# Seven block products in place of eight in the second product of the second layer's MLP, in token order

## The chip, the cores and the metric

The kernel runs on one core of a Trainium2 chip. The metric is the device time of one execution in microseconds (us). Before the change the median of three runs is 1055.32 us. A core has TensorE (PE, matrix products; PEld is its loading of the stationary operand), VectorE (DVE), ScalarE (ACT), GpSimd (POOL), and SyncE (SP), whose queue issues nearly all transfers here. Each engine works through its own queue in order and waits at its head for what it needs from the others. Products go into PSUM, which the kernel uses as eight banks of 128 x 512 numbers of 32 bits.

## The reference

Two layers work on 512 tokens of 1024 features. The first mixes tokens by Fourier groups and attention, the second by pooling. After its mixer each layer has an MLP, and the change touches the second layer's only:

```python
def sq_relu_mlp(u, w1, w2):
    a = jnp.maximum(u @ w1, 0.0)
    return (a * a) @ w2

h = h + g1 * y
h = h + g2 * sq_relu_mlp(modulate(rms_norm(h, norm2_g[l]), sh2, sc2), w_mlp1[l], w_mlp2[l])
```

Here u is 512 x 1024, w1 is 1024 x 4096, w2 is 4096 x 1024, and g2 is a row of 1024 gates, the modulation row v = 5 of the layer. All data are float32. The result of the second layer is the output.

## The kernel before

**Tiling.** The stream h lies transposed in SBUF: eight tiles `hT[d]` of 128 features by 512 tokens. Each matrix operand is split into a high part that the fast matrix format holds exactly and a low part, the rest; a product is made of three (`mm3`, lines 99 to 103): high by high, high by low, low by high, into the same PSUM bank.

**MLP.** `mlp` (line 1305 on) goes over four chunks c4 of 1024 hidden columns. In each, the first product makes eight tiles of hidden features (q = 0 to 3, m = 0, 1), 24 matmuls each; `act` (lines 1296 to 1303) squares the positive part and splits it. The second product makes eight tiles d of output features: weights as the stationary operand, hidden tiles `ah` as the moving one. `add_h` (line 855) adds a finished bank times the gate to `hT[d]`. In the last chunk `emit` turns each finished tile back to token order, four transposes on TensorE, and stores it.

**Weights.** `Feed` loads pieces of 128 x 1024 numbers (512 KB) in the order of their use, at most `nr` = 4 at a time (`load`, line 145 issues). `one` takes the next one: ScalarE casts it to its high half (`wh`, line 167), VectorE subtracts to get the low half (`wl`, line 170). There is room for eight split pieces, five in one pool and three in another; `done` gives a place back when a product has been written out in the program. `tick`, called after every second step of a product and after each `act`, takes at most one piece of weights, and only one whose load was issued over 4 us before by the program's own count.

**Order.** `manual_schedule` makes each engine issue in the order in which the program is written. Nothing overtakes: what is written ahead on VectorE is done ahead on VectorE. PSUM banks come in three classes: "m" with three, "s" with three, "t" with two.

**Buffers.** After attention, pool `M` holds "v" 16 tiles (activations in two parts), "a", "x" (three scratch tiles), "y", "z" and the band table.

Of the kernel before, what the change touches and what calls it, by code (L numbers as in the profile page):

```python
# [27 lines left out]
# columns of the constant block  # L28
# [4 lines left out]
# token windows (first token, first output, end of outputs) of the pooling products  # L33
# [5 lines left out]
def body(ctx: ExitStack, tc: tile.TileContext, x, c, cx, c_ctx, w_mod, b_mod, norm1_g, norm2_g,  # L39
         w_in, w_four, q_g, k_g, rpb, w_out, w_pool, pool_scale, w1, w2, kconst, kfour, kband, out):  # L40
    nc = tc.nc
    # every engine issues in the order in which the program is written
# [22 lines left out]
    class Slots:  # L65
        """tiles by class; one class never waits for another"""
# [8 lines left out]
    # ---------------------------------------------------------------- small jobs between the large products  # L75
# [33 lines left out]
    # ---------------------------------------------------------------- weights  # L109
# [3 lines left out]
    class Feed:  # L113
        """4 KB pieces in the order of their use: weights, which become two exact halves, and modulation rows, which are
        accumulated off the tensor engine"""

        def __init__(self, nr):
# [8 lines left out]
            # slow: the low parts of weights wait for a later moment  # L126
# [6 lines left out]
        def w(self, key, src, a, b):  # L133
            self.items.append(["w", key, src, (P, a, b), None, 0.0])
# [18 lines left out]
        def one(self, kind, auto=True, eng=None):  # L153
            """takes the next piece of a kind; nothing when there is none or no room for it"""
            if not self.wait[kind]:
                return False
            _, key, _, shape, raw, _ = it = self.wait[kind][0]
            if kind == "w":
                room = [h for h in self.halves if h[1] > 0]
# [6 lines left out]
                self.wait[kind].pop(0)  # L166
                nc.scalar.copy(hi, raw)  # L167

                def low():
                    (eng or nc.vector).tensor_tensor(lo, raw, hi.bitcast(F32), op=ALU.subtract)  # L170
# [9 lines left out]
            else:  # L180
                self.mac(key, raw)
                it[4] = None
# [6 lines left out]
        def beat(self):  # L189
            """what has had the time to arrive"""  # L190
# [22 lines left out]
        def need(self, l, v):  # L213
            """the columns of a modulation row, now"""
# [21 lines left out]
        def finish(self):  # L236
            (l, v), self.fin = self.fin, None
            ps = bank("t", "pmv")
# [5 lines left out]
            later(lambda: self.columns(l, v, ms), 7.0 if l or v == 5 else 1.5)  # L244

# [16 lines left out]
    W = Feed(4)  # L262
# [41 lines left out]
    # ---------------------------------------------------------------- constants and small parameters  # L304
# [42 lines left out]
    # silu of both conditioning vectors  # L347
# [9 lines left out]
    # ---------------------------------------------------------------- norms  # L357
# [6 lines left out]
    def rows(r, n):  # L364
        """token values in columns -> the same row on every partition"""
# [18 lines left out]
    # ---------------------------------------------------------------- transposed residual stream  # L384
# [29 lines left out]
    # ---------------------------------------------------------------- first modulation, in column chunks  # L414
# [19 lines left out]
    def mod_cols(j, ms):  # L434
# [3 lines left out]
        # md[j][:, block, shift or scale, token kind]  # L438
# [19 lines left out]
    # GEMM operands in window order: token = 128 * (column block) + 16 * row + column in block  # L458
# [83 lines left out]
    # ---------------------------------------------------------------- remaining parameters  # L542
# [6 lines left out]
    # Fourier tables  # L549
# [7 lines left out]
    # relative position table, sheared over the 16 columns of a query block  # L557
# [10 lines left out]
    def head_sums(sqs):  # L568
        """1 / rms of every head of every token tile"""
# [1017 lines left out]
```

## Time and profile before

| | |
|---|---|
| median of three runs | 1055.32 us (1054.09 to 1056.67) |
| span of the profiled execution | 1051.1 us |
| mean granted TensorE clock | 0.993 |
| instructions | 14034 |
| second layer's MLP, about | 691 us to the end |
| second product of its first chunk | 738.26 to 781.78 us |

The span runs from the first to the last instruction of the one execution that was profiled; the timed runs contain what lies around it as well. Rows of a timeline give the start, the duration, the engine, the line, the operation with output and inputs, and in brackets the idle time ahead of it with what ended it. Rows of groups give busy time, mean nanoseconds of one, and idle time ahead of the group with what ended most of it. Matmuls overlap, so the distance between two starts says more than a duration.

### The profile page before, as it was taken

The numbers are of one execution on the slowest core, as the hardware profiler recorded it, in microseconds if no ns is written. First come the engines' busy times: TensorE is split into PE (matmuls) and PEld (weight loads), VectorE is DVE, ScalarE is ACT, GpSimd is POOL, SyncE is SP. The second block draws the span as 40 slices with busy tenths as digits, with TensorE's granted clock in tenths as the row PEclk, the third lists the DMA queues.
The fourth block names the chain that finished last, engine by engine and source line by source line (L and its number), as shares of the span: only waits on it lengthen the run. The fifth ranks groups of instructions, "written<-read, shape, count | busy, mean of one in ns | idle before, by whom it ended". The sixth has DMA issues, their size and how long they took to land.

```text
span 1051.1 us, 14034 instructions
## 1 busy us (share of the span) xinstructions
PE 1020.8 (97%) x5449; PEld 846.6 (81%) x5449; DVE 598.6 (57%) x886; ACT 395.1 (38%) x695; POOL 101.0 (10%) x133
## 2 busy tenths in 40 slices
PE   6999999999899999999999999999999999999998
PEld 4688788776898777787888899988888888888887
DVE  5567767986866567757663434686334434434421
ACT  4264333675553124323412423665213313322310
POOL 1023103541410000000000001220000000000000
PEclk9999999999999999999999999999999999999999
DMA  9937645321426567767663220225232332332201
GB/s 301 325 106 228 222 156 164 92 48 57 124 74 203 189 221 237 239 221 235 201 203 121 81 81 1 62 80 177 84 113 88 92 109 80 105 96 83 78 25 56
DMA packets 106978, 143.46 MB, mean 136 GB/s; under 512 B 6197, under 2 KB 87749, under 8 KB 106911
## 3 DMA queue, kind: packets, MB, share of 16 engines
q1 hardware_dynamic: 106543, 141.95, 42.8%
q8 instruction: 43, 0.70, 0.3%
q0 software_dynamic: 368, 0.61, 0.2%
q14 instruction: 24, 0.20, 0.1%
HBM read 139.83 MB, written 2.70 MB: 136 GB/s over the span
## 4 chain that ended last, share of the span: by engine, by line
PE 71%; DMA 11%; DVE 10%; ACT 5%; issue 2%; SPq 0%; ACTq 0%; DVEq 0%
PE pw L100 17%; PE pw L102 17%; PE pw L101 17%; DMA wr<-in_w_mlp 8%; DVE wl L170 3%; ACT wh L167 3%; DMA wr<-in_w_in_even 2%; DVE macc L231 2%; PE pv L1016 1%; DVE sq L1172 1%; PE pt L996 1%; PE pwo L100 1%; PE pwo L101 1%; PE pwo L102 1%; PE pq L101 1%
## 5 line engine op out<-in xcount | busy, mean ns | idle before, releaser
L167 ACT CAST wh<-wr 128x1024 fp32r<-128x1024 f32 x158 | 162.6, 1046 | 268.4 <-PE pw L101 132.3
L170 DVE TENSOR_TENSOR wl<-wr,wh 128x1024 fp32r<-128x1024 f32 x147 | 176.3, 1222 | 78.1 <-ACT wh L167 74.9
L100 PE MATMUL pw<-ah,wh 128*128 128x512 f32 (+1 forms) x584 | 214.0, 366 | 1.6 <-ACT ah L1300 1.0
L102 PE MATMUL pw<-ah,wl 128*128 128x512 f32 (+1 forms) x584 | 212.4, 364 | 1.1 <-DVE wl L170 1.1
L101 PE MATMUL pw<-al,wh 128*128 128x512 f32 (+1 forms) x584 | 212.1, 363 | 1.0 <-DVE al L1302 1.0
L101 PE MATMUL pw<-vl,wh 128*128 128x512 f32 (+1 forms) x576 | 211.5, 367 | 1.2 <-ACT vl L1222 1.2
L100 PE MATMUL pw<-vh,wh 128*128 128x512 f32 (+1 forms) x576 | 212.5, 369 | 0.0
L102 PE MATMUL pw<-vh,wl 128*128 128x512 f32 (+1 forms) x576 | 211.3, 367 | 0.0
L100 PEld LDWEIGHTS pw<-ah,wh 128*128 128x128 f32 x584 | 110.2, 189 | 20.8 <-ACT wh L167 1.5
L102 PEld LDWEIGHTS pw<-ah,wl 128*128 128x128 f32 x584 | 110.2, 189 | 19.2 <-DVE wl L170 1.9
L101 PEld LDWEIGHTS pw<-al,wh 128*128 128x128 f32 x584 | 110.3, 189 | 18.0 <-DVE al L1302 1.3
L101 PEld LDWEIGHTS pw<-vl,wh 128*128 128x128 f32 x576 | 109.4, 190 | 19.0 <-ACT vl L1222 1.8
L100 PEld LDWEIGHTS pw<-vh,wh 128*128 128x128 f32 x576 | 109.4, 190 | 18.9 <-issue 1.6
L855 DVE SCALAR_TENSOR_TENSOR h<-pw,mv,h 128x512 f32<-128x512 f32 (+1 forms) x73 | 49.8, 683 | 131.2 <-PE pw L102 131.1
L102 PEld LDWEIGHTS pw<-vh,wl 128*128 128x128 f32 x576 | 109.3, 190 | 17.6
L1301 DVE TENSOR_TENSOR a<-a 128x512 f32<-128x512 f32 x64 | 44.1, 690 | 113.8 <-ACT a L1299 113.8
L1299 ACT ACTIVATE a<-pw 128x512 f32<-128x512 f32 x64 | 38.2, 597 | 160.4 <-PE pw L102 159.9
L231 DVE SCALAR_TENSOR_TENSOR macc<-wr,sil,macc 128x1024 f32<-128x1024 f32 x70 | 90.1, 1287 | 12.1 <-DMA wr<-in_w_mod 11.8
L1302 DVE TENSOR_TENSOR al<-a,ah 128x512 fp32r<-128x512 f32 x64 | 44.3, 693 | 7.0 <-DVE a L1301 0.5
L1300 ACT ACTIVATE ah<-a 128x512 fp32r<-128x512 f32 x64 | 40.5, 633 | 2.0
L1165 ACT ACTIVATE sq<-h 128x256 f32<-128x256 f32 x48 | 19.5, 415 | 48.0 <-DVE h L855 47.2
L1172 POOL TENSOR_TENSOR sq<-sq,sq 128x256 f32<-128x256 f32 x5 | 4.0, 808 | 333.6 <-ACT sq L1165 333.6
(237 smaller groups left out, 1261.6 us busy)
## 6 DMA issues: line engine op xcount, KB each, us to landing
wr<-in_w_mlp SPq DMA_DIRECT2D x128, 512.0 KB, 4.7
wr<-in_w_mod SPq DMA_DIRECT2D x80, 512.0 KB, 4.5
wr<-in_w_in_even SPq DMA_DIRECT2D x20, 512.0 KB, 5.4
wm<-in_w_mod SPq DMA_DIRECT2D x32, 256.0 KB, 7.2
wr<-in_w_out_even SPq DMA_DIRECT2D x8, 512.0 KB, 3.6
xn<-in_x SPq DMA_DIRECT2D x8, 256.0 KB, 5.0
out<-o SPq DMA_DIRECT2D x7, 256.0 KB, 2.3
tb<-dtab SPq DMA_DIRECT2D x64, 24.0 KB, 1.7
```

The lines of the kernel that those rows point to most:

```text
L100: nc.tensor.matmul(ps, lh, rh, start=start, stop=False)
L101: nc.tensor.matmul(ps, lh, rl, start=False, stop=False)
L102: nc.tensor.matmul(ps, ll, rh, start=False, stop=stop)
L167: nc.scalar.copy(hi, raw)
L170: (eng or nc.vector).tensor_tensor(lo, raw, hi.bitcast(F32), op=ALU.subtract)
L231: nc.vector.scalar_tensor_tensor(self.acc, w[:, 0, :], sil[:, k:k + 1], self.acc, op0=ALU.mult, op1=ALU.add)
L855: nc.vector.scalar_tensor_tensor(hT[d][:, c0:c1], ps[:, p0:p0 + c1 - c0], gate[:, d:d + 1], hT[d][:, c0:c1], op0=ALU.mult, op1=ALU.add)
L1165: nc.scalar.activation(self.sq, src, AF.Square)
L1299: nc.scalar.activation(a, ps, AF.Relu)
L1300: nc.scalar.activation(th, a, AF.Square)
L1301: nc.vector.tensor_tensor(a2, a, a, op=ALU.mult)
L1302: nc.vector.tensor_tensor(tl, a2, th.bitcast(F32), op=ALU.subtract)
```

## The change

The second layer's second product is read as one of two by two blocks. Rows of the result are the two halves of the tokens, columns the two halves of the output features; the inner dimension is split into the two halves of the hidden columns. Seven block products with sums and differences of blocks replace eight, chunk by chunk: a chunk is now 512 hidden columns of each half (`half_columns`). The stationary operand is a block of activations, hidden by tokens, and the moving one is 512 output columns of w2, so the result stands in token order in banks of 128 tokens by 512 features.

Per chunk: `act` makes the positive part and its square into one tile E of seven places; `sums` makes four combinations on VectorE, after q = 1 for the first half of the hidden rows (jj = 0) and after q = 3 for the second; `parts` splits a place in two. `Feed` gets roles: a "hold" piece stays in its raw buffer, an "add" piece is added to it on VectorE ahead of the split, and "keep" lets the total stand for a later addition. A chunk takes 18 weight pieces, made into 14, where it took eight. `nr` becomes 5. Banks are added into five token-order sums `ac`; in the last chunk `base` brings in the stream by transposes and the gate, and finished parts are stored from there. The gate is needed as a row on all partitions, so `row` makes it in place of `columns` for modulation row (1, 5). Pool `M` is divided: what only the earlier stages need lies in `Y`, and E and the sums take its place. The scratch for software-made transfers is set to 2048 bytes.

```diff
@@ Feed.one
+                keep = False
+                if role:
+                    _, place, keep = role
+                    total = self.kept[place][4]
+                    nc.vector.tensor_tensor(total, total, raw, op=ALU.add)
+                    raw = total
+                    self.out -= 1
+                    if not keep:
+                        self.kept.pop(place)
                 nc.scalar.copy(hi, raw)
 
                 def low():
                     (eng or nc.vector).tensor_tensor(lo, raw, hi.bitcast(F32), op=ALU.subtract)
-                    it[4] = None
-                    self.out -= 1
+                    if not keep:
+                        self.out -= 1
...
-    W = Feed(4)
+    W = Feed(5)
...
-    M = Slots(ctx, "my", {"v": 16, "a": 6, "x": 3, "y": 6, "z": 4, "bd": 1})
+    M = Slots(ctx, "my", {"v": 12, "a": 6, "x": 3})
...
+    PRODUCTS = ("11", "T3", "21", "T1", "T2", "T4", "22")
...
+                    parts = {"T1": [(0, 0, ("hold", ("a", q))), (0, 1, ("add", ("a", q), True))],
+                             "T2": [(1, 1, ("add", ("a", q), True))],
+                             "T4": [(1, 0, ("add", ("a", q), False))],
+                             "T3": [(0, 1, ("hold", ("c", q))), (1, 1, ("add", ("c", q), False))]}[name]
...
-    mlp(1, pair, slot_b, nB, emit, None, [lambda n=n: rest(n) for n in (3,2,0,0)])
+    def mlp_blocks(l, v, nB, between):
+        def sums(jj):
+            def tt(o, a, b, op):
+                nc.vector.tensor_tensor(two(o, jj), two(a, jj), two(b, jj), op=op)
+            tt(S1, A22, S3, ALU.subtract)
+            tt(S3, A11, S3, ALU.subtract)
+            tt(S2, S1, A11, ALU.add)
+            tt(S4, S2, A12, ALU.subtract)
+
+        def parts(name, jj):
+            hi, lo = M("v", "sh", F32R), M("v", "sl", F32R)
+            split(two(left[name], jj), hi, lo)
+            sp.setdefault(name, {})[jj] = (hi, lo)
+
+        def product(name, pss, cont, i_first=True, last=None):
+            order = ([(i, j) for i in range(2) for j in range(4)] if i_first else
+                     [(i, j) for jj in range(2) for i in range(2) for j in (2 * jj, 2 * jj + 1)])
+            for i, j in order:
...
+                nc.tensor.matmul(ps, lh, rh, start=not go, stop=False, skip_group_check=cont)
+                nc.tensor.matmul(ps, lh, rl, start=False, stop=False, skip_group_check=cont)
+                nc.tensor.matmul(ps, ll, rh, start=False, stop=j == 3, skip_group_check=cont)
+                if j % 2:
+                    tick()
+                if last and j == 3:
+                    last(i)
...
+        def base(acc, i, t, b, op):
+            gs = gate[:, 512 * b:512 * b + 512]
+            ps = bank("t", "pht")
+            for k in range(4):
+                nc.tensor.transpose(ps[:, k * P:(k + 1) * P], hT[4 * b + k][:, t * P:(t + 1) * P], ident)
+            nc.vector.tensor_tensor(acc[:, i, :], acc[:, i, :], gs, op=ALU.mult)
+            nc.vector.tensor_tensor(acc[:, i, :], ps, acc[:, i, :], op=op)
...
+                    for m in range(2):
+                        ps = bank("m", "pw1")
+                        w1_mm(ps, c4, q, m, 0, N)
+                        act(ps, q, m)
+                        if m:
+                            free("w1", c4, q)
+                        tick()
+                if q % 2:
+                    sums(q // 2)
+                    for name in PRODUCTS[0:3]:
+                        parts(name, q // 2)
+                if final and q < 2:
+                    for i in range(2):
+                        if q == 0:
+                            base(ac[0], i, i, 0, ALU.add)
+                            nc.vector.tensor_tensor(ac[3][:, i, :], ac[1][:, i, :], ac[3][:, i, :], op=ALU.add)
+                            base(ac[3], i, 2 + i, 1, ALU.subtract)
+                        else:
+                            nc.vector.tensor_tensor(ac[2][:, i, :], ac[1][:, i, :], ac[2][:, i, :], op=ALU.add)
+                            base(ac[2], i, 2 + i, 0, ALU.add)
+                            nc.vector.tensor_tensor(ac[4][:, i, :], ac[1][:, i, :], ac[4][:, i, :], op=ALU.add)
+                            base(ac[4], i, i, 1, ALU.subtract)
...
+            A = banks("mm")
+            product("11", A, False, i_first=False)
+            for i in range(2):
+                into(ac[1], i, A[i], fresh=c4 in (0, 3))
+            more("T1")
+            C = banks("ss")
+            product("T3", C, False, last=sum_c)
+            more("T2")
+            product("21", A, True, last=sum_a)
+            more("T4")
+            Dk = banks("ms")
+            product("T1", Dk, False, last=sum_d)
+            more("22")
+            B = banks("mm")
+            product("T2", B, False, last=sum_b)
+            product("T4", C, True, last=lambda i: (out_of(C, 2, i, 2 + i, 0, g0, ALU.add) if final else
+                                                  into(ac[2], i, C[i], fresh=c4 == 0)))
+            product("22", Dk, True, last=lambda i: (out_of(Dk, 4, i, i, 1, g1, ALU.subtract) if final else
+                                                   into(ac[4], i, Dk[i], fresh=c4 == 0)))
```

`sum_c`, `sum_a`, `sum_d` and `sum_b` evict a finished bank into a sum, one VectorE addition each outside the last chunk; with `fresh` the eviction is a copy on ScalarE. In the last chunk `sum_c` and `sum_d` gather a scratch tile, `sum_a` multiplies by the gate, adds and stores, `sum_b` is four VectorE operations and a store for each of its two banks, and `out_of` three and a store. `more` calls `parts` for both halves of a place.

More of the change, by code (lines that the diff above doesn't have):

```diff
@@ L125, in __init__ @@
             self.hold = False
+            self.kept = {}
             self.eng = None
@@ L131, in pool, with w, held @@
             self.halves.append([Slots(stack, name, {"wh": nh, "wl": nh}), nh])
-        def w(self, key, src, a, b):
-            self.items.append(["w", key, src, (P, a, b), None, 0.0])
+        def w(self, key, src, a, b, role=None):
+            self.items.append(["w", key, src, (P, a, b), None, 0.0, role])
+        def held(self):
+            while self.wait["w"] and self.wait["w"][0][6] and self.wait["w"][0][6][0] == "hold":
+                it = self.wait["w"].pop(0)
+                self.kept[it[6][1]] = it
         def m(self, l, v):
@@ L153, in one @@
         def one(self, kind, auto=True, eng=None):
+            if kind == "w":
+                self.held()
             if not self.wait[kind]:
                 return False
-            _, key, _, shape, raw, _ = it = self.wait[kind][0]
+            _, key, _, shape, raw, _ = it = self.wait[kind][0][0:6]
             if kind == "w":
+                role = self.wait[kind][0][6]
                 room = [h for h in self.halves if h[1] > 0]
@@ L189, in beat @@
         def beat(self):
+            self.held()
             for kind in ("w", "m"):
@@ L237, in finish @@
             (l, v), self.fin = self.fin, None
+            if (l, v) == (1, 5):
+                return self.row(l, v)
             ps = bank("t", "pmv")
@@ L244, in finish, with row @@
             later(lambda: self.columns(l, v, ms), 7.0 if l or v == 5 else 1.5)
+        def row(self, l, v):
+            pss = [bank("t", "pmv") for _ in range(2)]
+            for ps, hf in zip(pss, range(2)):
+                nc.tensor.matmul(ps, ones, self.acc[:, 512 * hf:512 * hf + 512], start=True, stop=True)
+            r = tp.tile([P, D], F32, tag="macc", name=nm("mrow"), bufs=1)
+            nc.sync.dma_start(r, b_mod[l:l + 1, D * v:D * (v + 1)].to_broadcast([P, D]))
+            for hf in range(2):
+                cs = slice(512 * hf, 512 * hf + 512)
+                nc.vector.tensor_tensor(r[:, cs], pss[hf], r[:, cs], op=ALU.add)
+            mv[l, v] = r
         def columns(self, l, v, ms):
@@ L1134, in body @@
     mix.close()
-    M = Slots(ctx, "my", {"v": 16, "a": 6, "x": 3, "y": 6, "z": 4, "bd": 1})
+    M = Slots(ctx, "my", {"v": 12, "a": 6, "x": 3})
     W.pool(ctx, "wy", 3)
+    tail = ctx.enter_context(ExitStack())
+    Y = Slots(tail, "mz", {"v": 4, "y": 6, "z": 4, "bd": 1})
     W.gap = 1e9
@@ L1145, in body @@
     turn_a = [1, 0, 1, 1, 0, 1, 0, 1, 1, 0, 1, 0, 1, 1, 0, 1]
+    turn_v = [0, 0, 0, 1]
     def slot_v(s, dt=F32R):
-        return M("v", s, dt)
+        turn_v.append(turn_v.pop(0))
+        return (Y if turn_v[-1] else M)("v", s, dt)
     class Norm:
@@ L1512, in body @@
     W.one("w", eng=nc.gpsimd)
-    def emit(d, c0, c1):
-        n = (c1 - c0) // P
-        ps = bank("t", "pout")
-        for t in range(n):
-            nc.tensor.transpose(ps[:, t * P:(t + 1) * P], hT[d][:, c0 + t * P:c0 + (t + 1) * P], ident)
-        o = M("x", "o")
-        if d % 2 and d < KT - 1:
-            nc.vector.tensor_copy(o[:, 0:c1 - c0], ps[:, 0:c1 - c0])
-        else:
-            nc.scalar.copy(o[:, 0:c1 - c0], ps[:, 0:c1 - c0])
-        nc.sync.dma_start(out[0, c0:c1, d * P:(d + 1) * P].rearrange("(t p) n -> p t n", p=P),
-                          o[:, 0:c1 - c0].rearrange("p (t n) -> p t n", t=n))
@@ L1534, in _constants @@
+    mlp_blocks(1, pair, nB, [lambda n=n: rest(n) for n in (3, 2, 0, 0)])
 def _constants():
```

158 lines of the change are left out of this document (145 added, 13 removed).

## The prediction

> **What bounds the kernel now.** I read the page first, then the windows over the second layer's MLP, then the timeline where its two products meet.
>
> ```profile
> span 1051.1 us, 14034 instructions
> PE 1020.8 (97%) x5449; PEld 846.6 (81%) x5449; DVE 598.6 (57%) x886; ACT 395.1 (38%) x695; POOL 101.0 (10%) x133
> PE 71%; DMA 11%; DVE 10%; ACT 5%; issue 2%; SPq 0%; ACTq 0%; DVEq 0%
> 738.26:781.78 43.52, 43.52 (x194) 36.04 (x192) 15.80 (x17) 10.51 (x11) 0.00 (x0) 1.00 0.32 97
> ```
>
> TensorE has work 97% of the span and carries the chain that ended last. The fourth line is the window of one chunk's second product (columns: window, its length, busy time of PE, PEld, DVE, ACT, POOL, granted clock, DMA share, GB/s): 192 weight loads in 43.52 us, so 0.2267 us a matmul at clock 1.00, never idle, with VectorE busy for 15.80 us. Here a matmul less is 0.2267 us less, while the other engines stay in time.
>
> **What is removed.** A chunk's 8 x 8 x 3 = 192 matmuls become 7 x 2 x 4 x 3 = 168, all 512 columns wide: a product is 24 matmuls, 5.44 us, and seven are 38.1 us. Four chunks lose 96 matmuls, 21.8 us.
>
> **What is added.** Per chunk: weight pieces made into halves rise from 8 to 14, each a ScalarE cast and a VectorE subtraction, and 8 block additions of 128x1024 come before them on VectorE; eight sums of activations, 14 splits of 128x512, 14 evictions into token-order sums. The prices:
>
> ```profile
> L170 DVE TENSOR_TENSOR wl<-wr,wh 128x1024 fp32r<-128x1024 f32 x60 | 70.7, 1219 | 2.4 <-ACT wh L167 0.5
> L167 ACT CAST wh<-wr 128x1024 fp32r<-128x1024 f32 x60 | 61.0, 1047 | 98.3 <-PE pw L101 98.3
> L1302 DVE TENSOR_TENSOR al<-a,ah 128x512 fp32r<-128x512 f32 x32 | 22.2, 693 | 3.3
> L1524 ACT COPY o<-pout 128x512 f32<-128x512 f32 x4 | 2.3, 587 | 39.3 <-PE pout L1519 39.3
> 836.60 0.75 DVE L855 SCALAR_TENSOR_TENSOR h<-pw,mv,h 128x512 f32<-128x512 f32 x1 [4.69 <-PE pw L102]
> 837.27 2.35 DVE L170 TENSOR_TENSOR wl<-wr,wh 128x1024 fp32r<-128x1024 f32 x2
> 1040.77 0.69 DVE L1522 COPY o<-pout 128x512 f32<-128x512 f32 x1 [5.66 <-PE pout L1519]
> 1041.37 0.74 DVE L855 SCALAR_TENSOR_TENSOR h<-pw,mv,h 128x512 f32<-128x512 f32 x1
> 315.97 0.68 DVE L1301 TENSOR_TENSOR a<-a 128x512 f32<-128x512 f32 x1
> 316.75 0.69 DVE L1302 TENSOR_TENSOR al<-a,ah 128x512 fp32r<-128x512 f32 x1
> ```
>
> Start to start on VectorE: 0.61 for 512 elements (1040.77 to 1041.37), 0.79 when the next reads the result (315.97 to 316.75), 0.66 out of PSUM (836.60 to 837.27), 1.14 for 1024 (two in 2.35). A block addition is not in the trace; it has L170's operands and size, so I price it 1.22.
>
> The decisive point is order. Within `one`, the addition, the cast of its sum on ScalarE and the subtraction stand one behind the other, and VectorE issues in program order. Addition 1.22, handover 0.05, cast 1.05, handover 0.03, subtraction 1.14: VectorE is held for 3.5 us by each added piece, two of them beside each product of 5.44 us. The bounds for one are 2.3 (nothing waits) and 3.5; I take 3.5, since nothing can pass.
>
> **The start of the seven products.** The chunk's last `act` is followed by `free` and a tick, and the tick takes a weight piece before `sums` is written.
>
> ```profile
> 999.60 0.39 PE L100 MATMUL pw<-ah,wh 128*128 128x512 f32 x1
> 999.80 0.60 ACT L1299 ACTIVATE a<-pw 128x512 f32<-128x512 f32 x1 [4.18 <-PE pw L102]
> 1000.43 0.63 ACT L1300 ACTIVATE ah<-a 128x512 fp32r<-128x512 f32 x1
> 1000.97 1.04 ACT L167 CAST wh<-wr 128x1024 fp32r<-128x1024 f32 x1
> 1002.04 2.36 DVE L170 TENSOR_TENSOR wl<-wr,wh 128x1024 fp32r<-128x1024 f32 x2
> ```
>
> The trace of before has this very order: from the first matmul of the second product (999.60, my zero below), the cast starts at 1.37 and the subtraction at 2.44. Behind it now stand the four sums (3.58, 4.19, 4.80, 5.59) and only then the low half that "11" needs (6.20, ready 6.89). The first half of "11" covers 12 x 0.2267 = 2.7 us and two more matmuls can go; ten remain at 7.0. "11" ends at 9.3 where 5.4 was due: **3.9 us lost, in each of four chunks**.
>
> **The bank that "T2" needs.** Its two "m" banks are those of "11" and "21", and come free when `sum_a` has read them on VectorE. Eight places for halves set which piece is taken when: "11", "T3", "21" are ready at the start, "T1" is taken at the start, "T2" beside "T3", "T4" beside "21". VectorE's queue from 6.20, chunks 1 and 2 (starts): splits of "T3", "21" 6.81, 7.42; T1's second piece 8.03 (3.5 long); evictions of A 11.52, 12.18; splits of "T1" 12.84, 13.45; T2's pieces 14.06, 17.55; `sum_c` 21.04, 21.70; splits of "T2" 22.36, 22.97; T4's pieces 23.58, 27.07; `sum_a` 30.56, done 31.25. TensorE: "T3" from 9.3, "21" 14.7, "T1" 20.2, finished at 25.6. "T2" starts at 31.3: **5.7 us lost**. Behind it all is in time ("22" needs its split at 42.2, it is there by 39). The seven end at 47.6 instead of 43.5. Behind the waiting VectorE instructions stand evictions and splits, and for those TensorE waits.
>
> In chunk 0 three pairs of evictions go to ScalarE as copies (0.59): two pairs, 2.64 us, leave VectorE ahead of that point, and the bank is free after a ScalarE copy at 27.4. Loss 1.8, end 43.75. In chunk 3 one pair goes (1.32): "T2" starts at 30.0, "22" ends at 46.3.
>
> **The tail.** In chunk 3 VectorE has after `sum_a`, splits, T-halves and `sum_d` until 38.1: `sum_b` twice 2.72, then four times 2.24 for `out_of`, so it ends at 52.5, six us behind TensorE. What follows the last result, before:
>
> ```profile
> 1047.96 0.37 ACT L1524 COPY o<-pout 128x256 f32<-128x256 f32 x1 [0.44 <-PE pout L1519]
> out<-o SPq DMA_DIRECT2D x7, 256.0 KB, 2.3
> ```
>
> The copy ends at 1048.33, the span 2.8 later. So 52.5 + 2.8 = 55.3, against 1051.1 - 999.6 = 51.5 now: +3.8, matmuls saved included.
>
> **`base` in chunk 3.** After q = 0 and after q = 1 four `base` calls each put four transposes into one of two "t" banks; the third must wait until VectorE has read the first bank, and the next first product stands behind it on TensorE.
>
> ```profile
> 1039.84 0.39 PE L102 MATMUL pw<-ah,wl 128*128 128x512 f32 x1
> 1040.08 0.60 PE L1519 MATMUL pout<-kc,h 128*128 128x128 f32 x4
> 1040.43 0.36 PE L100 MATMUL pw<-ah,wh 128*128 128x256 f32 x1
> ```
>
> Four transposes cost about 0.45 in the stream, as the old output ones did. At q = 0 VectorE comes from a subtraction at 2.44: multiply 3.58, add 4.37 (done 5.06), sum 4.98, multiply 5.77, add 6.56 (done 7.25); the fourth group runs 7.3 to 7.75. At q = 1 the sums and three splits of the first half stand before: sum 8.03, multiply 8.82, add 9.61, sum 10.22, multiply 11.01, add 11.80, done 12.5; TensorE goes on at 13.0. **Together 20.75 us** of which the old transposes were 3.6, still inside the 51.5.
>
> **The clock.**
>
> ```profile
> 695.25 0.28 PE L102 MATMUL pw<-vh,wl 128*128 128x256 f32 x1
> 696.28 1.50 PE L1182 MATMUL pss<-kc,sq 128*128 128x1 f32 x12 [0.76 <-DVE sq L1172]
> ...
> 699.29 0.41 PE L101 MATMUL pw<-vl,wh 128*128 128x256 f32 x1
> 699.50 0.41 PE L102 MATMUL pw<-vh,wl 128*128 128x256 f32 x1
> ...
> 702.43 0.28 PE L101 MATMUL pw<-vl,wh 128*128 128x256 f32 x1
> 702.55 0.28 PE L102 MATMUL pw<-vh,wl 128*128 128x256 f32 x1
> 700.00:705.00 5.00, 5.00 (x35) 5.00 (x35) 4.30 (x11) 4.96 (x12) 2.28 (x3) 0.77 0.00 0
> ```
>
> After a nearly empty stretch (12 one-column products), 256-column matmuls came at 0.21 instead of 0.12 from 699.07 to 702.27, 16 of them, at clock 0.77: 1.5 us lost. I charge 1.5 for the long waits: `base` twice, "T2" in chunks 1 and 2, 6 us. After the start wait it only shortens the wait at "T2", and chunk 3's T2 has VectorE's tail behind it. [...]
>
> **Elsewhere.** The fifth raw buffer loads one piece further ahead in all stages.
>
> ```profile
> PE pmv L240 <- DVE macc L231: 3.6, 4, 1.7
> PE pw L102 <- DVE wl L170: 1.1, 2, 0.5
> PE pw L100 <- ACT wh L167: 0.6, 1, 0.6
> 479.14 0.64 PE L240 MATMUL pmv<-macc,kc 128*32 128x256 f32 x8 [0.22 <-DVE macc L231]
> wr<-in_w_mlp SPq DMA_DIRECT2D x128, 512.0 KB, 4.7
> ```
>
> At most these 5.3 us of waits go; another order of arrival could cost as much. I take -2. The row `mv[1, 5]` replaces four products side by side (0.64) by two of 512 columns in sequence: 0 to +2, I take +1. Stores are eight instead of nine, with nothing behind them on SP's queue. The 40 further weight pieces (20 MB) go beside 390 us of a DMA that is a third busy; a piece lands in 4.7 us and is asked for over 8 us ahead, so nothing.
>
> **Sum.** Chunk 0 +0.2; chunks 1 and 2 2 x 4.1 = +8.2; chunk 3 +3.8; `base` +20.75; clock +6; elsewhere -1: +38, on a span of 1051.1, so 1089. The runs lie 4.2 above the span (1055.3 against 1051.1): **1093 us**.
>
> **Rivals.** *Faster, cover holds.* If pieces are taken earlier than I read (room for 8 halves, one piece a tick) VectorE reaches `sum_a` by 25.6, 5 us sooner, and the sums come before the piece: that is the point where it turns. Three chunks gain 5.4 each; chunk 3 would end 38.1 + 2.2 + 2.8 = 43.1 after its start, gaining 8.4; four transposes eight times cost 3.6: 1055.3 - 16.3 - 8.4 + 3.6 = 1034. For it: VectorE is busy for 15.8 of 43.5 now. Against: the order of rows at 999.60 to 1002.04. [...] 10%.
> *Half the waits.* Either the "T2" waits are missing (VectorE 1.1 quicker per added piece: 5 x 1.1 = 5.5): -1.8, 2 x -7.2 and some -1, 17 less, 1076; or the `base` waits are (their multiplications far ahead of the transposes): -17 and -3 clock, 1073. 22%.
> *Weights late.* Two held pieces leave three of five raw buffers. A buffer's turn is landing plus 3.5; the six pieces of "T2", "T4" and "22" take two turns, 16.4 us at 4.7, against 16.3 of three products. The slowest row of landings,
>
> ```profile
> wm<-in_w_mod SPq DMA_DIRECT2D x32, 256.0 KB, 7.2
> ```
>
> would make 21.4, so 5 us late in each chunk: 1113. Against: 4.7 holds for the MLP's own pieces. 12%.
> *No change* would need waits of just 21 us: 4%. That fewer matmuls aren't issued is excluded by the loops.
>
> **Numbers.** Forecast 52%. The likeliest case alone reaches from 1084 to 1102 (the -5 to +5 and clock bounds). From the middle case, both halves of it in part, to late weights: 1060 to 1114. Faster by over 0.2% (about what a measurement of this kernel can tell from none) 10%, within 4%, slower 86%.
>
> **What would show it.** Right: 168 matmuls a chunk, TensorE idle about 3.6 us before the second half of "11" on a VectorE subtraction; 4 to 6 us before "T2" on `sum_a`; over 9 us at `base` transposes; VectorE last at the end. Wrong: VectorE idle when "T1" ends, or `base` transposes without a wait.

## The result, and the profile after

The changed kernel takes **1093.84 us** (median of four runs, 1091.59 to 1095.69) against 1054.88 us for the kernel before, measured beside it: a ratio of 1.037, 95% interval 1.035 to 1.040. It is 39 us slower.

From the page of the kernel after: the span, the busy times, the granted clock in 40 slices, and the group of VectorE's weight subtractions.

```profile
span 1089.8 us, 14070 instructions
PE 1018.4 (93%) x5323; PEld 838.9 (77%) x5323; DVE 700.9 (64%) x1013; ACT 450.7 (41%) x781; POOL 100.6 (9%) x132
PEclk9999999999999999999999999999998999997899
L191 DVE TENSOR_TENSOR wl<-wr,wh 128x1024 fp32r<-128x1024 f32 x172 | 207.3, 1224 | 195.1 <-ACT wh L188 194.0
```

TensorE has 126 operations fewer and is busy for 2.4 us less, in a span that is 38.7 us longer: its share falls from 97% to 93%. VectorE has 102 us more work, and that is still only 64% of the span. The clock shows an 8 in the slice around 830 us, where chunk 1's second product lies, and a 7 and an 8 around 1000 us, in chunk 3. In the last row 172 subtractions stand behind 194 us of idle time that ended with ScalarE's cast: part of it is VectorE with nothing to do, part of it held by that cast. No engine is full; the time is in waits. Which ones, the view of TensorE's waits says (what waited, on whom; us in total, times, longest):

```profile
PE pht L1664 <- DVE acc L1666: 15.3, 4, 9.3
PE pw L1634 <- DVE sl L97: 13.1, 4, 3.3
PE pw L1632 <- ACT wh L188: 9.4, 3, 3.9
```

These are the transposes of `base`, the start of the second half of "11", and the start of "T2". None of them is in the kernel before. That they make 37.8 us together, close to the 39, is chance: 21.8 us of matmuls went as well, and transposes, a low clock and a longer tail came.

The windows of the kernel after, one a stage: the second product of chunks 0, 1 and 2, the first product of chunk 3, and the last second product with all that follows (window, length, busy PE, PEld, DVE, ACT, POOL, granted clock, DMA share, GB/s).

```profile
738.29:782.66 44.37, 40.58 (x170) 32.44 (x168) 34.08 (x38) 25.49 (x36) 0.00 (x0) 0.96 0.49 150
826.18:873.75 47.57, 41.46 (x169) 33.17 (x168) 39.10 (x47) 22.41 (x28) 0.00 (x0) 0.93 0.47 145
917.27:966.18 48.91, 41.70 (x170) 33.35 (x168) 39.10 (x47) 22.39 (x28) 0.00 (x0) 0.93 0.47 150
966.18:1035.27 69.09, 53.74 (x226) 43.73 (x225) 32.41 (x41) 17.07 (x24) 0.00 (x0) 0.85 0.27 93
1035.27:1089.80 54.53, 40.74 (x169) 32.26 (x167) 42.59 (x56) 16.10 (x23) 0.00 (x0) 0.92 0.22 77
```

The weight loads are 168 in each product, as the loops say, and VectorE went from 15.8 us to 39.1 in the middle chunks. Before, the first four stages took 43.52 us each and the last 51.5. The window of the kernel before for the stage that loses most, the first product of chunk 3:

```profile
956.08:999.60 43.52, 43.52 (x193) 36.04 (x192) 19.79 (x23) 15.32 (x21) 0.00 (x0) 1.00 0.24 73
```

So the differences are +0.85, +4.05, +5.4, +25.6 and +3.0; with 0.2 gained earlier, these are the 38.7. (The second product of chunk 0 starts at 738.29; before, its first matmul starts at 738.48, one matmul behind the 738.26 of the table.)

### The profile page after: what moved, and what is told of

The parts are those of the page before. It is cut to its first block, busy times and chain, and to the rows that moved or that the text cites. A ratio compares the mean times of both kernels' runs of the same rounds, so it can differ in the third digit from the quotient of the medians.

```text
span 1089.8 us, 14070 instructions
## 1 busy us (share of the span) xinstructions
PE 1018.4 (93%) x5323; PEld 838.9 (77%) x5323; DVE 700.9 (64%) x1013; ACT 450.7 (41%) x781; POOL 100.6 (9%) x132
## 4 chain that ended last, share of the span: by engine, by line
PE 70%; DVE 13%; DMA 8%; ACT 6%; issue 2%; SPq 0%; ACTq 0%; DVEq 0%
PE pw L100 12%; PE pw L101 12%; PE pw L102 12%; DMA wr<-in_w_mlp 7%; PE pw L1634 4%; PE pw L1632 3%; PE pw L1633 3%; ACT wh L188 3%; DVE wl L191 3%; DVE macc L252 2%; PE pv L1051 2%; DVE E L1608 1%; DVE sq L1212 1%; DVE sl L97 1%; PE pwo L100 1%
## 5 line engine op out<-in xcount | busy, mean ns | idle before, releaser
L188 ACT CAST wh<-wr 128x1024 fp32r<-128x1024 f32 x182 | 187.2, 1046 | 259.4 <-DMA wr<-in_w_mlp 105.9
L101 PE MATMUL pw<-al,wh 128*128 128x512 f32 (+1 forms) x320 | 112.6, 352 | 1.8 <-DVE al L1370 1.7
L100 PE MATMUL pw<-ah,wh 128*128 128x512 f32 (+1 forms) x320 | 113.4, 354 | 0.5 <-ACT ah L1368 0.5
L102 PE MATMUL pw<-ah,wl 128*128 128x512 f32 (+1 forms) x320 | 112.0, 350 | 0.0
L1634 PE MATMUL pw<-wh,sl 128*128 128x512 f32 x224 | 91.2, 407 | 13.1 <-DVE sl L97 13.1
L1632 PE MATMUL pw<-wh,sh 128*128 128x512 f32 x224 | 91.2, 407 | 10.1 <-ACT wh L188 9.4
L1633 PE MATMUL pw<-wl,sh 128*128 128x512 f32 x224 | 90.6, 404 | 0.0
L101 PEld LDWEIGHTS pw<-al,wh 128*128 128x128 f32 x320 | 61.4, 192 | 10.2 <-DVE al L1370 2.5
L100 PEld LDWEIGHTS pw<-ah,wh 128*128 128x128 f32 x320 | 61.2, 191 | 9.5 <-issue 1.1
L102 PEld LDWEIGHTS pw<-ah,wl 128*128 128x128 f32 x320 | 61.5, 192 | 7.8
L1632 PEld LDWEIGHTS pw<-wh,sh 128*128 128x128 f32 x224 | 44.4, 198 | 22.6 <-ACT sh L96 12.6
L1599 ACT ACTIVATE a<-pw 128x512 f32<-128x512 f32 x32 | 19.1, 596 | 88.7 <-PE pw L102 88.7
```

The costliest lines, as they stand in the source:

```text
L100: nc.tensor.matmul(ps, lh, rh, start=start, stop=False)
L101: nc.tensor.matmul(ps, lh, rl, start=False, stop=False)
L102: nc.tensor.matmul(ps, ll, rh, start=False, stop=stop)
L1599: nc.scalar.activation(a, ps, AF.Relu)
L1632: nc.tensor.matmul(ps, lh, rh, start=not go, stop=False, skip_group_check=cont)
L1633: nc.tensor.matmul(ps, lh, rl, start=False, stop=False, skip_group_check=cont)
```

## The experiments

Two explanations were set against each other. **Theory A** is that of the prediction: VectorE's order puts a handful of instructions in front of what TensorE needs, at three places (`base`, the start, "T2"). **Theory B** says that the places are only where a general shortage shows, of VectorE's time or of the weights' arrival, so that lifting one wait would move it to the next; what each means for a run stands in its expectation. Each of the first five runs changes one thing alone, the next two measure a term of the forecast, and then the edits are put together. All ratios are to the kernel before, run beside on the same chip; 1 us is 0.00095.

### `base` spread over the first product

The eight units of `base` leave their two blocks and stand two by two behind the first tile of each q; `some_bases(2)` writes the next two.

```diff
                         act(ps, q, m)
                         if m:
                             free("w1", c4, q)
                         tick()
+                        if final and not m:
+                            some_bases(2)
...
-                if final and q < 2:
-                    for i in range(2):
...
```

> Only the place of the eight base calls in the last chunk changes: two after the first act of each q, instead of four after q = 0 and four after q = 1. Theory A (TensorE waits at base because the third group of transposes needs a bank that VectorE has yet to read, behind sums and splits): the last chunk's first product falls from 69.1 us to about 47.1 (43.5 of matmuls and 3.6 of transposes), the rest stays, total about 22 us less than the changed kernel, 1072. Theory B (VectorE simply has too much to do in the last chunk): the same additions and multiplications push the sums and splits back, at most 10 us are won, and the waits at the start of the seven products or at T2 grow in that chunk.

Measured: 1072.0 us (1071.43 to 1072.56), ratio 1.018 [1.016, 1.020], 22 us less than the change by the medians and 20 by the ratios. The timeline of this kernel has all its transposes like this:

```profile
985.44 1.03 PE L1664 MATMUL pht<-kc,h 128*128 128x128 f32 x8
```

There are four such pairs of groups and no wait at any of them. The first product of chunk 3 takes 47.1 us, which is the old 43.5 plus 3.6 for 32 transposes. That stage alone gives 22.0 us (69.1 to 47.1), and the last stage stayed at 54.7. Theory A. The second product of chunk 1 took 49.2 us here instead of 47.6; it lies ahead of the edit, so this is how far one stage can differ between two executions.

### The sums ahead of the weight piece

```diff
-                        tick()
+                        if not (m and q % 2):
+                            tick()
                 if q % 2:
                     sums(q // 2)
                     for name in PRODUCTS[0:3]:
                         parts(name, q // 2)
+                    tick()
```

> Only the weight piece that is taken after the last act of q = 1 and q = 3 changes place: behind sums and splits instead of ahead of them. Theory A (VectorE's queue order makes both waits): the first sum starts at about 1.5 instead of 3.6 us, the wait before the second half of 11 falls by about 2 us in each chunk, but VectorE, not TensorE, sets when T2 starts, and its work ahead of that grows by nothing and shrinks only by the 1 us it stood waiting for the cast: 1 us less per chunk in chunks 1 to 3 and up to 2 in chunk 0, 3 to 5 us in total, 1089 to 1091. Theory B (the two waits are separate losses that add up): 4 x 2 = 8 us less, 1086.

Measured: 1102.76 us (1101.13 to 1103.77), ratio 1.047 [1.045, 1.049]: **slower** by 9 us, against both theories. Two rows of TensorE's timeline in chunk 1, whose second product starts at 829.82 here, show the start of the second half of "11" and that of "T2".

```profile
834.72 0.51 PE L1634 MATMUL pw<-wh,sl 128*128 128x512 f32 x1 [1.56 <-DVE sl L97]
862.39 0.77 PE L1632 MATMUL pw<-wh,sh 128*128 128x512 f32 x1 [7.72 <-ACT wh L188]
```

The start wait did fall, from 3.27 us to 1.56. But "T2" starts 32.57 us after the product's start where it was 31.15, and the reason stands on VectorE (the first sums, then, behind the splits, the addition and the subtraction of the moved piece):

```profile
831.32 2.75 DVE L1608 TENSOR_TENSOR E<-E 128x512 f32<-128x512 f32 x4 [5.86 <-ACT E L1601]
835.79 1.22 DVE L183 TENSOR_TENSOR wr<-wr,wr 128x1024 f32<-128x1024 f32 x1
838.12 1.23 DVE L191 TENSOR_TENSOR wl<-wr,wh 128x1024 fp32r<-128x1024 f32 x1 [1.12 <-ACT wh L188]
```

In the change the addition of that piece and the wait for its cast lay in the idle time before the sums, where VectorE waited for the last `act` anyway (the 5.86 in the first row). Moved as a whole, the piece brings 1.2 us of addition and 1.1 us of waiting into the busy stretch, ahead of `sum_a`. The clock added the rest. From the start of the second half of "11" to the wait at "T2" TensorE takes 19.95 us (834.72 to 854.67) in place of 21.43, so that more of the waiting falls at "T2" (7.72 us instead of 2.75), and behind that wait the clock is low (0.50 from 862.4 to 866.0, 0.73 from there to 870): from the start of "T2" to the next stage it takes 19.1 us in place of 16.4. The edit shortened a wait that was hidden behind another one, and lengthened the other.

### The addition stays, only the split moves

The same, but the block addition is made before the sums (`plus` does it once), and only cast and subtraction come after.

```diff
                 if q % 2:
+                    W.held()
+                    W.first()
                     sums(q // 2)
```

> As x2_sums_first, but the one addition that belongs to the moved weight piece stays ahead of the sums, where VectorE stands idle. Theory A (VectorE's queue sets T2's start; x2 lost because it moved that addition, 1.2 us, and the wait for its cast, 1.1, from idle time into the busy stretch): first sum at 1.5, wait before the second half of 11 about 1.6 us, T2 starts near 30.2 us after the products' start, against 31.2 in the changed kernel and 32.6 in x2; what the start gains the longer wait at T2 takes back, and more where the clock is halved after it: 1088 to 1096. Theory B (the sums' place as such is what costs): near x2, 1102.

Measured: 1089.77 us (1088.88 to 1093.86), ratio 1.035 [1.032, 1.037]. "T2" begins 30.23 us after the start of chunk 1 (826.57):

```profile
831.47 0.50 PE L1647 MATMUL pw<-wh,sl 128*128 128x512 f32 x1 [1.57 <-DVE sl L97]
856.80 0.77 PE L1645 MATMUL pw<-wh,sh 128*128 128x512 f32 x1 [6.46 <-ACT wh L189]
```

So it was the place of the addition that cost: it alone makes the difference of 2.3 us at "T2" between these two kernels (1.2 of addition, 1.1 of waiting). A gain over the change is not shown, as the interval overlaps the 1.035 to 1.040 of the change: what the start wait lost, the wait at "T2" took on (6.46 us where it was 2.75).

### Other banks for "T2"

```diff
-            B = banks("mm")
+            B = banks("tt")
```

> Only the banks of T2 change: the two of class t, which nothing uses in this stage, instead of those of 11 and 21. Theory A (T2 waits for sum_a to read its banks, as forecast): the wait at T2 goes in all chunks; T4's split is then late by 1 to 2 us instead; 3 to 4 us less in each of chunks 1 and 2, 1 to 2 in chunk 0, in the last chunk nothing since VectorE ends last there: 8 to 10 us in total, 1084 to 1086. Theory B (T2 waits for the high half of its weights, which the trace names): no change, 1094.

Measured: 1082.88 us (1079.9 to 1084.74), ratio 1.028 [1.026, 1.031], 10 us less. The second products of chunks 1 and 2 fall from 47.57 and 48.91 to 44.4 and 44.8. The waits of TensorE in this kernel:

```profile
PE pht L1664 <- DVE acc L1666: 15.3, 4, 9.3
PE pw L1634 <- DVE sl L97: 13.1, 4, 3.3
```

The wait at "T2" is gone from the list, although the view of the kernel after named a weight cast (`ACT wh L188`) as its end and no cast was touched. A wait for several things is put down to the one that came last by the profile, and here that name was wrong: only the bank was changed, so it was the bank that was missing.

### The next addition ahead of the cast's wait

Here the pieces keep their order, but the addition of the following piece is put on VectorE while ScalarE casts the sum of the present one.

```diff
-                    nc.vector.tensor_tensor(total, total, raw, op=ALU.add)
+                    self.plus(full)
+                    self.ahead(place)
                     raw = total
```

> Only the block additions of weights move: each is written one piece ahead, so that VectorE adds the next piece while ScalarE casts this one. The amount of work is the same. Theory A (VectorE is held 1.1 us by every cast of a sum, and that is what makes T2 late): T1's two additions fall into idle time, T2's and T4's pairs take 4.6 instead of 7 us, sum_a comes near 23, ahead of TensorE, and the wait at T2 goes; the wait at the start stays at 3.3 and with it the halved clock. About 4 to 5 us less in chunks 1 and 2, 1 in chunk 0, 5 in the last, whose end TensorE sets again: 1077 to 1081. Theory B (VectorE has too much to do, whatever the order): less than 5 us won, 1089 or more.

Measured: 1077.75 us (1074.5 to 1080.51), ratio 1.022 [1.020, 1.025], 16 us less. TensorE's waits:

```profile
PE pht L1689 <- DVE acc L1691: 15.3, 4, 9.3
PE pw L1659 <- DVE sl L97: 13.1, 4, 3.3
```

Again nothing at "T2", this time with its old banks: VectorE was late at `sum_a` mainly by the waits for its own casts, and not by its work, of which there is as much as in the change (1013 instructions in both). In chunk 1, which starts at 827.34 here, `sum_a` begins 24.06 us after the start where it was 30.32:

```profile
851.40 1.29 DVE L1679 TENSOR_TENSOR acc<-pw,acc 128x512 f32<-128x512 f32 x2
```

The five waits for casts ahead of it in the change make 5.7 of these 6.3 us. The rest is a second addition that now lies ahead of the sums, less a new wait of 0.65 us. Beside this, the last stage falls from 54.5 to 49.05: VectorE ran behind there too.

### A fifth raw buffer in the kernel before

```diff
-    W = Feed(4)
+    W = Feed(5)
...
-    nc = bacc.Bacc("TRN2", target_bir_lowering=False, num_devices=1)
+    nc = bacc.Bacc("TRN2", target_bir_lowering=False, num_devices=1, dynamic_dma_scratch_size=2048)
```

> The kernel before with five raw weight buffers and the small scratch, nothing else of the change. Theory A (the fifth buffer does next to nothing by itself): within 1 us of before, 1055. The forecast's own term: 2 us less, 1053. Theory C (it costs, by another order of arrival): 2 to 5 us more.

Measured: 1052.74 us (1047.81 to 1054.18), ratio 0.999 [0.998, 1.0005]: this cannot be told from no change, though up to 2.5 us less lie within the interval. The row on which the prediction put its hope is longer here than the 3.6 us before:

```profile
PE pmv L240 <- DVE macc L231: 5.3, 3, 2.3
```

### The waits filled with products

A direct measure of what the clock costs. Each long wait of TensorE is filled with matmuls into a bank that nobody reads; the real work is the same. The number in each place is that which fits into the wait.

```diff
+        def fill(n, tag):
+            ps = bank(tag, "pfill")
+            for _ in range(n):
+                nc.tensor.matmul(ps, vh[0][:, 0:P], vh[1], start=True, stop=True)
...
+                if name == "11" and (i, j) == (0, 2):
+                    fill(16, "s")
...
+                        if i:
+                            fill((17, 39)[q], "s")
...
+            fill((8, 23, 23, 18)[c4], "t")
             product("T2", B, False, last=sum_b)
```

> The changed kernel with its waits filled by products that nobody reads: 16 in the start wait of each chunk, 8, 23, 23 and 18 ahead of T2, 17 and 39 ahead of the third group of transposes in the two base stretches; each fill is as long as the wait it stands in, so that no instruction of use starts later for it. Theory A (the halved clock after long waits costs about 6 us, where the start wait's share is hidden by T2's wait): clock 1.00 through the second layer's MLP, 4 to 6 us less than the changed kernel, 1088 to 1090. Theory B (the clock term is worth nothing, as VectorE sets the times anyway): 1093 to 1095, or more where a fill is too long.

Measured: 1084.16 us (1082.79 to 1084.89), ratio 1.032 [1.029, 1.034]; against the ratio of the change, 0.0055 or 5.8 us less. In the windows of this kernel after the start wait of chunk 1 and after the wait at "T2" in chunk 2 the clock is full:

```profile
833.00:837.00 4.00, 4.00 (x19) 3.31 (x18) 2.88 (x4) 2.09 (x3) 0.00 (x0) 1.00 0.37 123
948.00:952.00 4.00, 4.00 (x19) 3.31 (x18) 4.00 (x6) 3.44 (x6) 0.00 (x0) 1.00 0.58 168
```

In the change it was 0.50 and 0.60 there:

```profile
833.10:837.00 3.90, 3.85 (x9) 3.07 (x10) 2.79 (x4) 1.53 (x2) 0.00 (x0) 0.50 0.11 20
948.40:952.00 3.60, 3.57 (x10) 2.89 (x11) 3.60 (x5) 3.60 (x6) 0.00 (x0) 0.60 0.61 200
```

By stages the full clock gave back 4.9 us in the first product of chunk 3 (69.1 to 64.2), 1.3 in chunk 2 and nothing in chunks 0 and 1: 6.2 us. In chunk 1 only 9 matmuls are run in some 4 us after the start wait where 19 are run at full clock (the first rows of the two pairs), but "T2" waits for VectorE in any case, so the slow matmuls only shorten that wait. The other 1.2 us by which this span is shorter lie before the first of these places.

### The edits together

First `base` is spread, additions are made one piece ahead, and the weight piece is taken behind the sums while its addition stays ahead of them; the split of the activations for "11" now comes ahead of the sums.

```diff
                 if q % 2:
+                    W.held()
+                    W.ahead(None)
+                    parts(PRODUCTS[0], q // 2)
                     sums(q // 2)
-                    for name in PRODUCTS[0:3]:
+                    for name in PRODUCTS[1:3]:
                         parts(name, q // 2)
+                    tick()
```

> Base spread over the last chunk, additions one piece ahead, and at the start the split for 11 ahead of the sums and the weight piece behind them (its addition ahead). Theory A (the three waits are all that stands against the 96 matmuls saved): no wait over 1 us in the seven products, 38.1 us each, and 43 to 44 for the last chunk with its tail: 20 us below the kernel before, 1031 to 1038. Theory B (a further limit, VectorE's load or weights that land late, appears when these go): 1045 or more, with a new wait on weights or on an eviction.

Measured: 1045.6 us (1043.46 to 1048.43), ratio 0.992 [0.990, 0.995]. It beats the kernel before, but stays 8 us above the upper end of theory A and lies where theory B put it: 1045 or more, with a new wait on an eviction. Two waits are left on TensorE in chunk 1, a new one on the eviction of "11" ahead of "21" and one at "T2", and the clock after the second is low (the window below them):

```profile
831.11 0.50 PE L1657 MATMUL pw<-wh,sh 128*128 128x512 f32 x1 [0.84 <-DVE acc L1679]
844.21 0.47 PE L1657 MATMUL pw<-wh,sh 128*128 128x512 f32 x1 [1.88 <-ACT wh L190]
```

```profile
844.00:848.00 4.00, 3.79 (x10) 3.00 (x11) 4.00 (x6) 3.92 (x6) 0.00 (x0) 0.58 0.84 273
```

The next kernel gives "T2" the "t" banks as well, and the one after it makes both of "T1"'s additions before the sums, so that one addition instead of two stands between the splits and the evictions of "11".

```diff
-            B = banks("mm")
+            B = banks("tt")
```

> x6_all_three with T2 on the two banks of class t. Theory A: if sum_a is in time in x6, the banks no longer matter: within 1.5 us of x6. If it is faster by 3 us or more, VectorE is still late at sum_a in x6.

```diff
                     W.ahead(None)
+                    W.second()
                     parts(PRODUCTS[0], q // 2)
```

> x10_all_and_banks with both additions for T1 ahead of the sums, where VectorE stands idle, instead of one. Theory A (VectorE's queue in the first three products is what is left): the wait of 0.8 us for the eviction of 11 in chunks 1 and 2 goes, VectorE's tail in the last chunk starts 1.2 us sooner: 2 to 4 us less, 1035 to 1037. Theory B (what is left is TensorE's own time): within 1 us of x10.

Measured: 1039.16 us (1038.56 to 1041.6), ratio 0.986 [0.984, 0.989], and 1035.98 us (1035.25 to 1038.01), ratio 0.985 [0.982, 0.987]. The first shows by its 6 us that in the kernel before it VectorE was still late at `sum_a`; 0.84 us ahead of "21" was left in it in chunks 1 and 2. By their times the two cannot be told apart, as their intervals overlap; what the second gains is read from the trace, where the second products of chunks 1 and 2 fall from 39.2 to 38.1 us. In it the seven products take 38.1 us in every chunk; chunks 0 and 1 as windows:

```profile
738.20:776.30 38.10, 38.10 (x170) 31.56 (x169) 32.65 (x37) 25.42 (x36) 0.00 (x0) 1.00 0.56 180
819.80:857.90 38.10, 38.10 (x170) 31.50 (x169) 35.92 (x44) 21.95 (x28) 0.00 (x0) 1.00 0.50 158
```

TensorE is busy for the whole of both, at full clock, with as many instructions on VectorE and ScalarE as in the change (1013 and 781 in the whole kernel). So neither VectorE's time nor the arrival of the weights was short, and theory B falls, though VectorE is busy for 35.9 of the 38.1 us in chunk 1. The order alone would probably not have done it, though no run shows it: `sum_a` of chunk 1 begins at 842.81, 23.0 us after the start, and TensorE comes to "T2" after four products, 21.8 us: by these rows "T2" would still wait about 2 us for its old banks.

Last, the tail. In the last chunk VectorE ends 6.0 us after the start of TensorE's last matmul (1030.48 against 1024.47). The eight final additions before the stores go to GpSimd, which has nothing to do there.

```diff
-                nc.vector.tensor_tensor(ac[a][:, i, :], ac[a][:, i, :], y, op=op)
+                nc.gpsimd.tensor_tensor(ac[a][:, i, :], ac[a][:, i, :], y, op=op)
```

> x11_both_adds_early with the eight final additions into the token-order sums of the last chunk on GpSimd instead of VectorE. Theory A (VectorE ends last in the last chunk): 8 x 0.7 us leave VectorE, TensorE sets the end again, and the last addition is 0.6 us longer on GpSimd: 2 to 3 us less than x11, 1032 to 1035. Theory B (the end hangs on what follows the last product): no gain or up to 1 us more.

Measured: 1034.85 us (1033.54 to 1037.95), ratio 0.984 [0.981, 0.987]: no gain that can be told from the kernel before it, and the last stage is 47.3 us where it was 46.9. Timeline of this kernel, VectorE:

```profile
1021.57 0.68 DVE L1835 TENSOR_TENSOR y<-pw,acc 128x512 f32<-128x512 f32 x1
1022.28 1.27 DVE L1836 TENSOR_TENSOR y<-y,mrow 128x512 f32<-128x512 f32 x1
1023.48 0.68 DVE L1835 TENSOR_TENSOR y<-pw,acc 128x512 f32<-128x512 f32 x1
```

and GpSimd:

```profile
1021.72 1.28 POOL L1837 TENSOR_TENSOR acc<-acc,y 128x512 f32<-128x512 f32 x1 [0.62 <-DVE y L1836]
```

VectorE's multiplication takes 1.27 us beside GpSimd's addition; on VectorE alone, in the kernel without this edit, it takes 0.69. One eviction costs 1.91 us start to start instead of 2.06, and the last addition then takes 1.26 on GpSimd instead of 0.69: the two nearly cancel.

## Why the prediction was right, point by point

**The order on VectorE** is the step that carries the rest, and it held within 0.3 us over 30 us. Chunk 1 of the kernel after, whose second product starts at 826.18; rows of VectorE, with the predicted start behind zero being 2.44, 3.58, 6.20, 8.03, 11.52 and 30.56:

```profile
828.61 1.23 DVE L191 TENSOR_TENSOR wl<-wr,wh 128x1024 fp32r<-128x1024 f32 x1 [7.07 <-ACT wh L188]
829.75 2.74 DVE L1608 TENSOR_TENSOR E<-E 128x512 f32<-128x512 f32 x4
832.41 1.89 DVE L97 TENSOR_TENSOR sl<-E,sh 128x512 fp32r<-128x512 f32 x3
834.21 1.22 DVE L183 TENSOR_TENSOR wr<-wr,wr 128x1024 f32<-128x1024 f32 x1
836.54 1.23 DVE L191 TENSOR_TENSOR wl<-wr,wh 128x1024 fp32r<-128x1024 f32 x1 [1.11 <-ACT wh L188]
837.69 1.28 DVE L1654 TENSOR_TENSOR acc<-pw,acc 128x512 f32<-128x512 f32 x2
...
856.50 1.28 DVE L1654 TENSOR_TENSOR acc<-pw,acc 128x512 f32<-128x512 f32 x2
```

Measured behind zero: 2.43, 3.57, 6.23, 8.03, 11.51 and 30.32. The idle 1.11 us in the row at 836.54 is VectorE held by the cast of its own sum: the added piece takes 3.5 us from 834.21 to 837.69, the upper of the two bounds, and the addition 1.22 as priced from the subtraction.

**The start and "T2".** TensorE in the same chunk, and in chunk 2 at "T2":

```profile
833.15 0.79 PE L1634 MATMUL pw<-wh,sl 128*128 128x512 f32 x1 [3.27 <-DVE sl L97]
...
857.33 0.47 PE L1632 MATMUL pw<-wh,sh 128*128 128x512 f32 x1 [2.75 <-ACT wh L188]
...
948.43 0.77 PE L1632 MATMUL pw<-wh,sh 128*128 128x512 f32 x1 [3.85 <-ACT wh L188]
```

The second half of "11" starts at 6.97 (predicted 7.0), "T2" at 31.15 (predicted 31.3). The wait shown at "T2" is 2.75 and not 5.7: half clock after the start wait (0.50 from 833.10 to 837), on which the prediction put nothing but a shorter wait there, used up the rest. So the sign of 4 to 6 us idle ahead of "T2" was missed (2.75, 3.85 and 2.75 us in chunks 1 to 3, and the view names a weight cast), while the start of "T2" was met. What counts, the stage, came out at +4.05 for a predicted +4.1 in chunk 1. In chunk 2 it was +5.4, the 1.4 above being clock (0.60 from 948.40 to 952). Chunk 0 was +0.85 instead of +0.2.

**`base`.** Rows of TensorE in chunk 3:

```profile
982.17 1.11 PE L1664 MATMUL pht<-kc,h 128*128 128x128 f32 x4 [4.07 <-DVE acc L1666]
984.29 1.11 PE L1664 MATMUL pht<-kc,h 128*128 128x128 f32 x4 [1.01 <-DVE acc L1666]
997.83 1.03 PE L1664 MATMUL pht<-kc,h 128*128 128x128 f32 x8
1008.12 1.11 PE L1664 MATMUL pht<-kc,h 128*128 128x128 f32 x4 [9.26 <-DVE acc L1666]
```

TensorE goes on with the first product at 985.05, 7.99 us after the first transpose (977.06), and at 1011.01, 13.18 after 997.83: together 21.2, predicted 20.75. Spreading the units gave the 22 us back and left the 3.6 of the transposes, which is the price taken from the old output transposes.

**The clock** is right in its sum by two errors that cancel. Six microseconds were charged, 3 at `base` and 3 at "T2". In the trace, the products after the two `base` blocks take 12.78 us (985.05 to 997.83, 48 matmuls, 10.88 at 0.2267) and 24.26 (1011.01 to 1035.27, 96 of them, 21.76), so 1.9 and 2.5 too long, 4.4 together (the clock was 0.52 from 985 to 989 and 0.50 from 1011 to 1014); chunk 2 has the 1.4 and chunk 1 nothing: 5.8. Filling the waits measured 6.2 by stages and 5.8 by the times. The charge of 1.5 per wait was too low at `base` and too high at "T2" of chunk 1. The clock bounds in the range of the likeliest case are the author's estimate: no run shows them, and filling the start wait of chunk 0 gave nothing back.

**The tail.** VectorE's last addition begins at 1086.08 and takes 0.69, so it ends 51.5 us after the stage's start, predicted 52.5; the stage lost 3.0 instead of 3.8.

**Elsewhere.** The -2 for the fifth raw buffer is not borne out: alone in the kernel before it gives a ratio of 0.999, within the noise, and the waits that it was to take away are still there. Earlier stages are 0.2 us shorter in all, where -1 was the sum.

**Luck.** That 1093 came within 1 us is in part chance. Chunk 0 was 0.65 us worse than its term and `base` 0.4, the tail was 0.8 better, and the gain put on the earlier stages fell short by 0.8; these errors have both signs and nearly cancel, as the two of the clock do.

**The rivals.** *Weights late* falls: in the last of the joined kernels the same pieces feed products that never wait. *Half the waits* falls: all three waits came. Spreading `base`, other banks and additions ahead each took one away without another of the three growing by as much; only the two runs that moved the sums ahead shortened the start wait and lengthened the one at "T2", behind which it was hidden. *Faster, cover holds* was wrong for this order of the program and right about what the products are worth: with the order changed and other banks for "T2", seven products take 38.1 us as its sum had it, and the kernel takes 1036 us where 1034 was worked out. The two numbers are nearer than the sums behind them: 1036 stands beside a kernel before of 1053, so 17 us are gained where the rival had 21. Three chunks gave their 16.3 and the transposes cost their 3.6, but the last stage took 46.9 us and not 43.1, as VectorE still ends last in it.

So 39 us slower is not the price of the seven products. The same arithmetic takes 1036 us in another order and with other banks, 1.5% less than the kernel before and 5% less than the change as it was made.

## What to carry to other kernels

Where a change takes work from the busiest engine and gives it to one with room, write down the second engine's queue in program order, with each start, from the first instruction of the stage to the first one that the busy engine needs; here plain additions gave each start within 0.3 us over 30, while the shares of busy time pointed the other way. A chain that goes from an engine to another and back (add, cast elsewhere, subtract) holds an in-order queue for the length of the other's work, here 1.1 us a time; putting the next piece's first step into that gap made the change 16 us faster here. And before moving an instruction, see whether it lies in idle time now: the run with the sums first lost 9 us, and 13 us lie between it and the run that left one addition where it had cost nothing.

## What the runs showed of the hardware

**The clock behind a wait.** The same wait of 3.27 us, on the same instruction, stands in all four chunks of the kernel after. The clock fell after each of them, but not in the same way. In chunk 1 matmuls came at 0.43 us, start to start, from the first one on and for 5 us (the window from 833.10 above, clock 0.50); windows behind the wait in chunks 0, 2 and 3, and behind the wait of 2.75 us at 857.33:

```profile
745.20:749.00 3.80, 3.74 (x11) 3.02 (x12) 2.69 (x5) 1.42 (x2) 0.00 (x0) 0.67 0.12 14
924.20:928.00 3.80, 3.76 (x10) 2.99 (x11) 2.69 (x4) 1.44 (x2) 0.00 (x0) 0.58 0.09 21
1042.20:1046.00 3.80, 3.76 (x11) 2.98 (x12) 2.69 (x4) 1.44 (x3) 0.00 (x0) 0.66 0.10 16
857.30:861.00 3.70, 3.67 (x16) 3.09 (x17) 3.70 (x5) 3.70 (x6) 0.00 (x0) 1.00 0.72 208
```

In chunk 2 the slow matmuls begin at once and last 3 us; in chunks 0 and 3 they begin more than 1 us behind the wait and last some 3.4 us. A wait of 2.75 us left the clock at 1.00, while 1.88 us in the kernel with three edits was followed by a window at clock 0.58, and 0.84 us by full clock (1.00 from 831 to 834). So the length alone does not decide. What else does, no run here shows.

**GpSimd beside VectorE.** The multiplication of 1.27 us above has both inputs in SBUF; the addition before it (`y<-pw,acc`), with one input in PSUM, stays at 0.68 us although the same GpSimd addition runs beside it from 1021.72. In the kernel without this edit the two take 0.69 and 0.68. So the one with both inputs in SBUF was slower beside GpSimd and the other was not; why, no run here shows.
